# RMSNorm with Silu on one core: Square, sum and gamma in operations of four rows, with rstd as the scale of one-row Silu

## The chip, the cores and the metric

The kernel runs on one core of a Trainium2 chip. The rounds of the experiments ran on three different chips, each beside the kernel before, so kernels of different rounds are best compared by their ratios. The metric is the time of one execution on the device in microseconds (us), as the median of the runs. Engines: ACT is ScalarE, DVE is VectorE, POOL is GpSimd, SP is SyncE, which issues the loads. The stores are issued from ACT.

## The reference

```python
# x: [16, 1024, 512] float32, gamma: ones(512), eps = 1e-5
rms = np.sqrt(np.mean(x ** 2, axis=-1, keepdims=True) + eps)
x_norm = x / rms * gamma
out = x_norm * (1.0 / (1.0 + np.exp(-x_norm)))        # Silu
```

That is 33.5 MB in and 33.5 MB out, and little arithmetic on each element.

## The kernel before

The 16,384 rows lie as 128 partitions x 128 rows. They come in tiles of 4, 4, 8, six times 16, 8 and 8 rows (per partition) into a ring of 96 rows, and are worked on in place, in 32 chunks of four rows. The schedule is written by hand: what stands in the loop is the order of each engine's instructions.

```python
def sums(k):                       # mean square: three rows on ACT, one on DVE
    for j in range(cn):            # cn = 4
        row = xb[:, chunks[k] + j, :]
        if j < n_act:              # n_act = 3
            nc.scalar.activation(out=junk, in_=row, func=AF.Square,
                                 accum_out=ms[:, k, j : j + 1])
        else:
            nc.vector.tensor_tensor_reduce(... accum_out=ms[:, k, j : j + 1])

def root(k):                       # DVE: mean + eps; POOL: to the power -0.5
    nc.vector.tensor_scalar(out=aeps[:, k, :], in0=ms[:, k, :], ...)
    nc.gpsimd.tensor_tensor(out=rstd[:, k, :], in0=aeps[:, k, :],
                            in1=neg_half[:], op=ALU.pow)

def norm(k):                       # DVE: x * rstd * gamma, row by row, in place
    for j in range(cn):
        nc.vector.scalar_tensor_tensor(out=row, in0=row,
            scalar=rstd[:, k, j : j + 1], in1=gamma_sb[:], ...)

def swish(k):                      # ACT: Silu of four rows in one operation
    nc.scalar.activation(out=rows, in_=rows, func=AF.Silu)

for k in range(K + 3):             # K = 32; [cut: guards]
    sums(k); root(k)
    # stores of finished tiles
    norm(k - 1)
    swish(k - 2)                   # and loads of further tiles
```

Of the kernel before, what the change touches and what calls it, by code (L numbers as in the profile page):

```python
# [1 line left out]

# [4 lines left out]


@with_exitstack
def kernel(  # L10
    ctx: ExitStack,
    tc: tile.TileContext,
    x: bass.AP,
    gamma: bass.AP,
    eps: bass.AP,
    out: bass.AP,
):
    nc = tc.nc
    P = nc.NUM_PARTITIONS
    AF = mybir.ActivationFunctionType  # L20
    ALU = mybir.AluOpType
    fp32 = mybir.dt.float32
    bf16 = mybir.dt.bfloat16

    xf = x.flatten_outer_dims()
    of = out.flatten_outer_dims()
    R, D = xf.shape


    sizes = [4, 4, 8] + [16] * 6 + [8, 8]  # L30
    ring = 96
    ahead = 32
    cn = 4
    n_act = 3
    N = sum(sizes)
    assert N * P == R, (N, R)


    tiles = []
    done = 0  # L40
    for sz in sizes:
        assert done % ring + sz <= ring
        tiles.append((done * P, sz, done % ring))
        done += sz
    chunks = [r for _, sz, at in tiles for r in range(at, at + sz, cn)]
    K = len(chunks)

    pool = ctx.enter_context(tc.tile_pool(name="all", bufs=1))
    junk_pool = ctx.enter_context(tc.tile_pool(name="junk", bufs=1))
    xb = pool.tile([P, ring, D], fp32, name="xb")  # L50
    gamma4 = pool.tile([P, D], fp32, name="gamma4")
    gamma_sb = pool.tile([P, D], fp32, name="gamma_sb")
    neg_half = pool.tile([P, cn], fp32, name="neg_half")
    ms = pool.tile([P, K, cn], fp32, name="ms")
    aeps = pool.tile([P, K, cn], fp32, name="aeps")
    rstd = pool.tile([P, K, cn], fp32, name="rstd")

    inv_d = 1.0 / float(D)
    eps_f = float(eps)

    def dram(ap, t):
        first, sz, _ = tiles[t]
        return ap[first : first + P * sz].rearrange("(p n) d -> p n d", n=sz)

    def buf(t):
        _, sz, at = tiles[t]
        return xb[:, at : at + sz, :]

    def load(t):
        nc.sync.dma_start(out=buf(t), in_=dram(xf, t))  # L70

    def store(t):
        nc.scalar.dma_start(out=dram(of, t), in_=buf(t))

    def sums(k):
        for j in range(cn):
            row = xb[:, chunks[k] + j, :]
            if j < n_act:
                junk = junk_pool.tile([P, D], bf16, name=f"junk_a{j}")
                nc.scalar.activation(  # L80
                    out=junk[:], in_=row, func=AF.Square,
                    accum_out=ms[:, k, j : j + 1],
                )
            else:
                junk = junk_pool.tile([P, D], bf16, name=f"junk_v{j}")
                nc.vector.tensor_tensor_reduce(  # L86
                    out=junk[:], in0=row, in1=row,
                    scale=1.0, scalar=0.0, op0=ALU.mult, op1=ALU.add,
                    accum_out=ms[:, k, j : j + 1],
                )  # L90

    def root(k):
        nc.vector.tensor_scalar(  # L93
            out=aeps[:, k, :], in0=ms[:, k, :], scalar1=inv_d, scalar2=eps_f,
            op0=ALU.mult, op1=ALU.add,
        )
        nc.gpsimd.tensor_tensor(  # L97
            out=rstd[:, k, :], in0=aeps[:, k, :], in1=neg_half[:], op=ALU.pow
        )

    def norm(k):
        for j in range(cn):
            row = xb[:, chunks[k] + j, :]
            nc.vector.scalar_tensor_tensor(  # L104
                out=row, in0=row, scalar=rstd[:, k, j : j + 1],
                in1=gamma_sb[:], op0=ALU.mult, op1=ALU.mult,
            )

    def swish(k):
        rows = xb[:, chunks[k] : chunks[k] + cn, :]  # L110
        nc.scalar.activation(out=rows, in_=rows, func=AF.Silu)  # L111

    with tc.manual_schedule():
        nc.gpsimd.memset(gamma4[:], 0.0)  # L114
        nc.gpsimd.memset(neg_half[:], -0.5)  # L115
        nc.scalar.dma_start(out=gamma4[0:P:32, :], in_=gamma.partition_broadcast(4))
        nc.scalar.preload_act_table_set("silu_and_others")  # L117

        loaded = 0
        rows_loaded = 0  # L120
        while rows_loaded < ahead:
            load(loaded)
            rows_loaded += tiles[loaded][1]
            loaded += 1

        ends = []
        e = 0
        for _, sz, _ in tiles:
            e += sz // cn
            ends.append(e)  # L130
        stored = 0
        for k in range(K + 3):
            if k < K:
                sums(k)
                root(k)
            while stored < len(tiles) and ends[stored] <= k - 2:
                store(stored)
                stored += 1
            if k == 0:
                nc.vector.stream_shuffle(gamma_sb[:], gamma4[:], [0] * 32)  # L140
            if 1 <= k <= K:
                norm(k - 1)
            if 2 <= k < K + 2:
                swish(k - 2)
                while loaded < len(tiles) and ends[loaded] <= k - 1 + ahead // cn + 2:
                    load(loaded)
                    loaded += 1


# [1 line left out]
_INS = ['x', 'gamma', 'eps']  # L151
_OUTS = [((16, 1024, 512), 'float32')]

_NUMBERS = {'eps': 9.999999747378752e-06}


# [26 lines left out]
```

## Time and profile before

| | before |
|---|---|
| median time | 163.06 us (three runs, 162.83 to 163.09) |
| span in the profile | 161.1 us |
| bytes moved, mean rate | 67.15 MB, 417 GB/s |
| DMA per chunk of four rows | 2.1 MB, about 5.0 us at that rate |
| compute per chunk while data is there | 3.64 us |

These are lines of the page of the kernel before: the busy time of each engine, then two rows of the 40 equal slices of the span (tenths busy of the DMA engines, and GB/s), then the line of the chain of waits that gives its parts by line (a q behind an engine's name means its queue of instructions).

```profile
DVE 110.7 (69%) x226; ACT 118.7 (74%) x225; POOL 46.4 (29%) x38
DMA  5999989999899999999999999999999999999993
GB/s 171 437 435 521 390 352 488 413 403 480 366 407 431 484 411 447 399 456 447 399 447 456 399 439 464 417 415 421 431 435 464 419 403 472 415 415 423 439 415 146
...
DMA xb<-in_x_dram 41%; DMA out_dram<-xb 19%; ACT junk_a L80 12%; ACT xb L111 8%; DVE xb L104 3%; SPq L70 1%; DVEq L178 0%; DVE aeps L93 0%; ACTq L80 0%
```

The DMA engines are at 8 tenths or more from the second slice to the last but one; the two compute engines are busy for about 70% only. The chain that ended last is mostly transfers. So DMA is the limit. The longest waits of ACT and DVE (engine, line and tile, what it waited for, us in total, times, longest) agree:

```profile
ACT junk_a L80 <- DMA xb<-in_x_dram: 23.9, 7, 6.9
DVE junk_v L86 <- DMA xb<-in_x_dram: 19.6, 5, 5.8
```

ACT and DVE stand still for loads for some 20 us each. The timeline shows what a chunk costs where data is there (start us, duration us, engine, line, operation, out<-in, shape, count; in brackets the idle time before it and what ended it). Here and below, lines that the reading does not need are left out between those shown. The first two lines are from the start of the kernel:

```profile
7.63 0.72 DVE L140 STREAM_SHUFFLE gamma_sb<-gamma 128x512 f32<-128x512 f32 x1
7.84 1.01 POOL L97 TENSOR_TENSOR rstd<-aeps,neg_half 128x4 f32<-128x4 f32 x1 [6.55 <-DVE aeps L93]
...
110.51 0.17 DVE L93 TENSOR_SCALAR aeps<-ms 128x4 f32<-128x4 f32 x1 [0.22 <-ACT junk_a L80]
110.59 2.73 DVE L104 SCALAR_TENSOR_TENSOR xb<-xb,rstd,gamma_sb 128x512 f32<-128x512 f32 x4
110.76 1.44 POOL L97 TENSOR_TENSOR rstd<-aeps,neg_half 128x4 f32<-128x4 f32 x1 [2.20 <-DVE aeps L93]
114.15 0.17 DVE L93 TENSOR_SCALAR aeps<-ms 128x4 f32<-128x4 f32 x1 [0.22 <-ACT junk_a L80]
```

The eps operation comes again after 114.15 - 110.51 = 3.64 us. Look also at the pow on POOL. Beside the shuffle, which has one input, it takes 1.01 us; beside the multiply by rstd and gamma, which has two inputs in SBUF (the on-chip memory of the operands), it takes 1.44 us. In this kernel nothing waits long for it.

### The profile page before, as it was taken

The page shows a single profiled execution, that of the slowest core. Times are in us where ns is not written, and L with a number is a line of the kernel's source. Part 1 is how long each engine was busy: PE and PEld are TensorE (multiplying, and loading weights), DVE is VectorE, ACT ScalarE, POOL GpSimd, SP SyncE. Part 2 cuts the span into 40 slices and gives each one's busy share as a digit, 9 for nine tenths or more (in the row PEclk, how much of TensorE's full clock was granted, in tenths as well). Part 3 has the DMA queues.
Part 4 walks back from the last instruction along what each step waited for, and adds up shares of the span by engine and source line. Part 5 has one row for each costly group of instructions (what it writes and reads, how often), then busy time and mean ns, then how long its engine had stood idle before and what let it go on. Part 6 is the DMA issues. An engine that isn't in the chain of part 4 may idle for free.

```text
span 161.1 us, 612 instructions
## 1 busy us (share of the span) xinstructions
DVE 110.7 (69%) x226; ACT 118.7 (74%) x225; POOL 46.4 (29%) x38
## 2 busy tenths in 40 slices
DVE  0376946998999999999966998069999604990000
ACT  3447919999999999999939996099999408954000
POOL 1052403333444433333333333033333302400000
DMA  5999989999899999999999999999999999999993
GB/s 171 437 435 521 390 352 488 413 403 480 366 407 431 484 411 447 399 456 447 399 447 456 399 439 464 417 415 421 431 435 464 419 403 472 415 415 423 439 415 146
DMA packets 3180, 67.15 MB, mean 417 GB/s; under 512 B 356, under 2 KB 356, under 8 KB 360
## 3 DMA queue, kind: packets, MB, share of 16 engines
q1 hardware_dynamic: 1584, 33.56, 49.1%
q10 hardware_dynamic: 1592, 33.56, 48.4%
q14 instruction: 4, 0.03, 0.0%
HBM read 33.56 MB, written 33.55 MB: 417 GB/s over the span
## 4 chain that ended last, share of the span: by engine, by line
DMA 59%; ACT 20%; another core or an unknown queue 4%; issue 4%; DVE 3%; SPq 1%; DVEq 0%; ACTq 0%
DMA xb<-in_x_dram 41%; DMA out_dram<-xb 19%; ACT junk_a L80 12%; ACT xb L111 8%; DVE xb L104 3%; SPq L70 1%; DVEq L178 0%; DVE aeps L93 0%; ACTq L80 0%
## 5 line engine op out<-in xcount | busy, mean ns | idle before, releaser
L104 DVE SCALAR_TENSOR_TENSOR xb<-xb,rstd,gamma_sb 128x512 f32<-128x512 f32 x128 | 87.4, 745 | 0.0
L80 ACT ACTIVATE junk_a<-xb 128x512 bf16<-128x512 f32 x96 | 59.0, 615 | 23.9 <-DMA xb<-in_x_dram 23.9
L97 POOL TENSOR_TENSOR rstd<-aeps,neg_half 128x4 f32<-128x4 f32 x32 | 45.6, 1426 | 94.1 <-DVE aeps L93 94.1
L111 ACT ACTIVATE xb<-xb 128x2048 f32<-128x2048 f32 x32 | 60.7, 1896 | 1.8 <-DVE xb L104 1.8
L86 DVE CUSTOM_DVE_ANT_0 junk_v<-xb 128x512 bf16<-128x512 f32 x32 | 21.9, 685 | 19.6 <-DMA xb<-in_x_dram 19.6
L80 ACT ACTIVATION_READ_ACCUMULATOR junk_a<-xb 128x1 f32 x96 | 18.0, 187 | 0.0
L93 DVE TENSOR_SCALAR aeps<-ms 128x4 f32<-128x4 f32 x32 | 5.4, 170 | 14.5 <-ACT junk_a L80 14.5
L117 ACT ACT_TABLE_LOAD x1 | 1.3, 1283 | 2.4 <-issue 2.4
L86 DVE DVE_READ_ACCUMULATOR2_ANT ms<- 128x1 f32 x32 | 2.6, 82 | 0.0
L140 DVE STREAM_SHUFFLE gamma_sb<-gamma 128x512 f32<-128x512 f32 x1 | 0.7, 725 | 0.0
L114 POOL MEMSET gamma<- 128x512 f32 x1 | 0.5, 524 | 0.3 <-POOLq L164 0.3
L164 POOL MEMSET const-float32-0.0<- 128x1 f32 x1 | 0.1, 98 | 0.2 <-issue 0.2
L164 POOL MEMSET const-bfloat16-1.0<- 128x1 bf16 x1 | 0.1, 101 | 0.0
L164 POOL MEMSET const-uint8-127<- 128x1 uint8 x1 | 0.1, 101 | 0.0
L115 POOL MEMSET neg_half<- 128x4 f32 x1 | 0.1, 101 | 0.0
L164 POOL MEMSET const-float32-1.0<- 128x1 f32 x1 | 0.1, 98 | 0.0
L140 DVE LOAD_MASK_SELECT gamma_sb<-gamma x1 | 0.0, 14 | 0.0
## 6 DMA issues: line engine op xcount, KB each, us to landing
xb<-in_x_dram SPq DMA_DIRECT2D x6, 4096.0 KB, 43.8
out_dram<-xb ACTq DMA_DIRECT2D x6, 4096.0 KB, 34.6
xb<-in_x_dram SPq DMA_DIRECT2D x3, 2048.0 KB, 38.8
out_dram<-xb ACTq DMA_DIRECT2D x3, 2048.0 KB, 13.9
xb<-in_x_dram SPq DMA_DIRECT2D x2, 1024.0 KB, 5.8
out_dram<-xb ACTq DMA_DIRECT2D x2, 1024.0 KB, 19.7
gamma<-in_gamma_dram ACTq DMA_DIRECT2D x1, 8.0 KB
```

Source lines behind the costliest of these rows:

```text
L70: nc.sync.dma_start(out=buf(t), in_=dram(xf, t))
L80: nc.scalar.activation(out=junk[:], in_=row, func=AF.Square, accum_out=ms[:, k, j : j + 1],)
L86: nc.vector.tensor_tensor_reduce(out=junk[:], in0=row, in1=row, scale=1.0, scalar=0.0, op0=ALU.mult, op1=ALU.add, accum_out=ms[:, k, j : j ...
L93: nc.vector.tensor_scalar(out=aeps[:, k, :], in0=ms[:, k, :], scalar1=inv_d, scalar2=eps_f, op0=ALU.mult, op1=ALU.add,)
L97: nc.gpsimd.tensor_tensor(out=rstd[:, k, :], in0=aeps[:, k, :], in1=neg_half[:], op=ALU.pow)
L104: nc.vector.scalar_tensor_tensor(out=row, in0=row, scalar=rstd[:, k, j : j + 1], in1=gamma_sb[:], op0=ALU.mult, op1=ALU.mult,)
L111: nc.scalar.activation(out=rows, in_=rows, func=AF.Silu)
L114: nc.gpsimd.memset(gamma4[:], 0.0)
L115: nc.gpsimd.memset(neg_half[:], -0.5)
L117: nc.scalar.preload_act_table_set("silu_and_others")
L140: nc.vector.stream_shuffle(gamma_sb[:], gamma4[:], [0] * 32)
L164: nc = _bacc.Bacc("TRN2", target_bir_lowering=False, num_devices=1)
```

## The change

The intent is to have fewer, larger operations: one Square of four rows on ACT into PSUM (a second on-chip memory), one sum of them on DVE, one multiply by gamma on DVE that no longer needs rstd, and rstd as the scale of Silu, which then runs row by row on ACT. It is meant to save the fixed cost of many small operations (before, a Square of 512 columns takes 615 ns on ACT, a Silu of 2048 columns 1896 ns, less than four times that) and of the accumulator reads (187 ns each on ACT, 96 of them). The loop's order is changed too: Square(k) now stands behind Silu(k-2) on ACT, where it stood behind Silu(k-3) before.

```diff
+    def square(k):
+        squares[k] = squares_pool.tile([P, cn, D], fp32, name="sq")   # PSUM, 2 buffers
+        nc.scalar.activation(
+            out=squares[k][:], in_=rows(k), func=AF.Square, scale=inv_d**0.5
+        )
     def sums(k):
-        for j in range(cn): ...            # three Squares on ACT, one on DVE  [cut]
+        nc.vector.tensor_reduce(
+            out=ms[:, k, :], in_=squares.pop(k)[:], op=ALU.add,
+            axis=mybir.AxisListType.X,
+        )
-    def norm(k):
-        for j in range(cn): ...            # row * rstd * gamma  [cut]
+    def scaled(k):
+        nc.vector.tensor_tensor(
+            out=rows(k), in0=rows(k),
+            in1=gamma_sb[:].unsqueeze(1).to_broadcast([P, cn, D]), op=ALU.mult,
+        )
     def swish(k):
-        nc.scalar.activation(out=rows, in_=rows, func=AF.Silu)
+        for j in range(cn):
+            row = xb[:, chunks[k] + j, :]
+            nc.scalar.activation(
+                out=row, in_=row, func=AF.Silu, scale=rstd[:, k, j : j + 1]
+            )
         for k in range(K + 3):
-            sums(k); root(k)
             # stores
-            norm(k - 1)
             swish(k - 2)                   # and loads
+            square(k)
+            scaled(k)
+            sums(k)
+            root(k)
```

## The prediction

> **What bounds the kernel now.** DMA. The slices show it 9 tenths busy or more nearly throughout; 67.15 MB at a mean 417 GB/s, so about 5.0 us per chunk of four rows. Compute is faster: with data there, the timeline repeats every 3.64 us per chunk, and the waits show ACT 23.9 us and DVE 19.6 us waiting for loads. Compute ends at 146.8 us, DMA 12 us later. So the question is only whether the new schedule still fits under 5.0 us per chunk.
>
> **Engine work per chunk, after (estimates).**
> ACT: Square of 2048 about 1.85 us (Silu of 2048 is 1.895 us now)[...].[...] Sum 4.3 us (3.64 before).
> DVE: multiply about 2.25 us, sum from PSUM about 2.3 us (scaled from one 512-column operation at 683 ns per step[...]), eps about 0.15 us: 4.65 us (3.6 before). Each engine alone would fit.
>
> **The chain does not fit.** In the new order Square(k) stands behind Silu(k-2) on ACT, and the in-place multiply waits for Square(k). So there is a loop over two chunks: Square 1.85, multiply 2.25, sum 2.3, eps 0.2, pow 1.0 to 1.44,[...] and some 0.3 us of handovers: 10.3 to 10.7 us, 5.15 to 5.35 us per chunk. That alone makes compute slower than DMA.
>
> **The pow may make it worse.** Now pow takes 1.012 us once, beside a one-input shuffle, and 1.439 us otherwise, when it starts 0.17 us into a 512-column multiply with two SBUF inputs: 0.43 us more[...].[...] the trace agrees with a block to the end of one instruction. The new multiply is four times as long: if every second pow begins just behind it, it waits about 2.0 us, takes about 3.0 us, and the loop grows to about 12.3 us, 6.1 per chunk. The other pow (DVE idle then) stays near 1.0.
>
> **Time.** First chunk at 5.5 us, 32 chunks of 6.1 us, the last chain, the last 2 MB store with nothing to hide it (estimate 7 us), 2 us between span and time: about 211 us with the block, 183 to 190 us without. I give the block two chances in three. Predicted 209 us, range 182 to 218. Chances: faster 0.01, same 0.03, slower 0.96.
>
> **What would show it right.** DMA no longer full in the slices, 320 to 370 GB/s; ACT's waits for loads nearly gone, in their place Silu waiting for pow and the multiply for Square; the chain of waits through ACT, DVE and POOL, not DMA; pow in two groups, about 1.0 and 3.0 us, if the block is real, or all 1.0 to 1.45 us if not; starts of the multiply alternating between 4.7 us and 7.6 us (block) or 5.6 us (no block).
>
> **What would make it wrong.**[...] Square and multiply overlapping;[...] a phase in which no pow meets a multiply. If DVE alone set the pace, 4.65 us per chunk, it would still be about 169 us.

Some sums hold a term that is no longer listed: ACT's 4.3 us per chunk is Square's 1.85 and an estimate for four Silu, and the loop's 10.3 to 10.7 us holds the same estimate; the terms left there come to 7.9 us with a pow of 1.0 and to 8.3 with 1.44. The changed kernel then showed 2.47 us from four Silu to the next Square. The scaling of DVE's 2.25 and 2.3 us took off a fixed part; a line through 170 ns for the 4 columns of eps and 683 ns for 512, both in the trace before, gives 2.23 us for 2048. The 0.3 us of handovers and the 7 us of the last store are estimates: before, a pow starts 0.08 us after the end of its eps (110.76 in the timeline above), and in the changed kernel the span ends 7.2 us after the issue of the last store (202.64 to 209.8). For the block there is what the one trace shows: the pow's 0.43 us more, counted from its start 0.17 us into the multiply, reach to 0.60 us, near the end of that multiply's step of 0.68 us. That the wait would grow with the multiply was the estimate.

## The result, and the profile after

The changed kernel takes 211.6 us (median of 4 runs, 211.57 to 211.61) against 163.07 us before (four runs: the three above and one more). The ratio is 1.298, 95% interval 1.296 to 1.300. Ratios here and below are the mean time of one kernel's runs over the mean of the other's of the same rounds, so they are not quite the ratio of the medians quoted. The result is correct.

The same lines of the page after:

```profile
DVE 148.4 (71%) x98; ACT 138.7 (66%) x161; POOL 64.5 (31%) x38
DMA  6999999999999999999999700990029600794727
GB/s 231 439 431 431 406 437 405 470 390 459 450 425 420 406 469 425 406 469 428 400 464 428 312 0 0 400 400 0 0 100 400 300 0 0 300 400 200 300 100 300
...
POOL rstd L97 23%; DVE xb L102 17%; ACT xb L110 17%; DVE ms L87 17%; ACT sq L82 13%; DMA gamma<-in_gamma_dram 2%; DVE aeps L93 1%; POOLq L179 1%; DVE gamma_sb L145 0%; POOL gamma L115 0%; DVEq L102 0%; POOL neg_half L116 0%; DVEq L145 0%; P
```

The change did not save work on the engines: instructions fell from 612 to 395, but DVE is busy for 148.4 us (110.7 before) and ACT for 138.7 (118.7 before). DVE now sums all four rows of a chunk instead of one, and ACT runs Silu row by row.

The DMA is full up to the 22nd slice; after that it has gaps, and the waits below show that compute sets them, not the loads. Over the whole span it moves 320 GB/s, where the prediction had said 320 to 370. The chain that ended last is now pow, multiply, Silu, sum and Square, with 13% to 23% each, and the transfers of x and out have left it (the page cuts this line at its end). The waits of ACT and DVE for this circle of work, and ACT's for loads:

```profile
ACT xb L110 <- POOL rstd L97: 58.9, 16, 5.3
DVE xb L102 <- ACT sq L82: 42.7, 15, 2.9
ACT sq L82 <- DMA xb<-in_x_dram: 2.5, 2, 1.8
```

Loads are hardly waited for. ACT's Silu waits for pow, and DVE's multiply waits for Square: 16 and 15 times, so in every second chunk. One turn of the timeline shows why:

```profile
114.89 1.86 ACT L82 ACTIVATE sq<-xb 128x2048 f32<-128x2048 f32 x1
116.68 2.54 ACT L110 ACTIVATE xb<-xb,rstd 128x512 f32<-128x512 f32 x4
116.78 2.29 DVE L102 TENSOR_TENSOR xb<-xb,gamma_sb 128x2048 f32<-128x2048 f32 x1 [2.85 <-ACT sq L82]
118.98 2.28 DVE L87 TENSOR_REDUCE ms<-sq 128x4 f32<-128x2048 f32 x1
121.30 0.17 DVE L93 TENSOR_SCALAR aeps<-ms 128x4 f32<-128x4 f32 x1
121.38 2.28 DVE L102 TENSOR_TENSOR xb<-xb,gamma_sb 128x2048 f32<-128x2048 f32 x1
121.55 2.98 POOL L97 TENSOR_TENSOR rstd<-aeps,neg_half 128x4 f32<-128x4 f32 x1 [6.54 <-DVE aeps L93]
124.56 2.56 ACT L110 ACTIVATE xb<-xb,rstd 128x512 f32<-128x512 f32 x4 [3.57 <-POOL rstd L97]
126.15 1.01 POOL L97 TENSOR_TENSOR rstd<-aeps,neg_half 128x4 f32<-128x4 f32 x1 [1.62 <-DVE aeps L93]
127.03 1.86 ACT L82 ACTIVATE sq<-xb 128x2048 f32<-128x2048 f32 x1
```

Follow the circle from one Square to the Square two chunks later, by differences of the starts: Square to multiply 1.89, to sum 2.20, to eps 2.32, to pow 0.25, pow until Silu 3.01, four Silu until the next Square 2.47. The sum is 12.14 us for two chunks, 6.07 per chunk, more than the 5.0 that DMA needs. No engine is full in it: DVE is busy for 71% of the span, ACT for 66%.

The pow in the circle takes 2.98 us, the other one, at 126.15, takes 1.01 us. The long one starts 0.17 us behind the start of the next chunk's multiply.

### The profile page after: what moved, and what is told of

The parts are those of the page before. It is cut to its first block, busy times and chain, and to the rows that moved or that the text cites. A ratio compares the mean times of both kernels' runs of the same rounds, so it can differ in the third digit from the quotient of the medians. Undisturbed runs are those within 1.5% of the kernel's fastest.

```text
span 209.8 us, 395 instructions
## 1 busy us (share of the span) xinstructions
DVE 148.4 (71%) x98; ACT 138.7 (66%) x161; POOL 64.5 (31%) x38
## 4 chain that ended last, share of the span: by engine, by line
DVE 36%; ACT 30%; POOL 23%; issue 5%; DMA 2%; POOLq 1%; DVEq 0%
POOL rstd L97 23%; DVE xb L102 17%; ACT xb L110 17%; DVE ms L87 17%; ACT sq L82 13%; DMA gamma<-in_gamma_dram 2%; DVE aeps L93 1%; POOLq L179 1%; DVE gamma_sb L145 0%; POOL gamma L115 0%; DVEq L102 0%; POOL neg_half L116 0%; DVEq L145 0%; POOLq L97 0%; POOLq L165 0%
## 5 line engine op out<-in xcount | busy, mean ns | idle before, releaser
L110 ACT ACTIVATE xb<-xb,rstd 128x512 f32<-128x512 f32 x128 | 81.6, 708 | 59.0 <-POOL rstd L97 58.9
L97 POOL TENSOR_TENSOR rstd<-aeps,neg_half 128x4 f32<-128x4 f32 x32 | 63.7, 1992 | 135.0 <-DVE aeps L93 135.0
L102 DVE TENSOR_TENSOR xb<-xb,gamma_sb 128x2048 f32<-128x2048 f32 x32 | 73.2, 2289 | 42.8 <-ACT sq L82 42.7
L87 DVE TENSOR_REDUCE ms<-sq 128x4 f32<-128x2048 f32 x32 | 73.1, 2283 | 0.0
L82 ACT ACTIVATE sq<-xb 128x2048 f32<-128x2048 f32 x32 | 59.5, 1859 | 2.5 <-DMA xb<-in_x_dram 2.5
```

The lines of the kernel that those rows point to most:

```text
L82: nc.scalar.activation(out=squares[k][:], in_=rows(k), func=AF.Square, scale=inv_d**0.5)
L87: nc.vector.tensor_reduce(out=ms[:, k, :], in_=squares.pop(k)[:], op=ALU.add, axis=mybir.AxisListType.X,)
L102: nc.vector.tensor_tensor(out=rows(k), in0=rows(k), in1=gamma_sb[:].unsqueeze(1).to_broadcast([P, cn, D]), op=ALU.mult,)
L110: nc.scalar.activation(out=row, in_=row, func=AF.Silu, scale=rstd[:, k, j : j + 1])
```

## The experiments

Two things are to be told apart. LOOP is the two-chunk circle. BLOCK is the idea that a pow which meets a multiply with two SBUF inputs must wait for this one instruction. The rivals are that pow is merely slowed while DVE works (SLOW), that only the sum of engine work counts (WORK), or that blocked pows cost time wherever they are. Twelve kernels were run, all correct, each in three timed rounds beside the kernel before.

| run | what differs from the changed kernel | median us | ratio to before |
|---|---|---|---|
| (changed) | | 211.60 | 1.298 |
| split13 | multiply in 1 + 3 rows | 188.88 | 1.158 |
| split22 | multiply in 2 + 2 rows | 196.89 | 1.207 |
| sqsbuf | squares as bf16 in SBUF | 212.09 | 1.301 |
| gammapsum | sqsbuf, and gamma in PSUM | 183.19 | 1.123 |
| lag3 | Silu one chunk later | 167.51 | 1.026 |
| sumsfirst | sum and eps ahead of the multiply | 178.46 | 1.093 |
| lag3_tail | lag3, last tile cut in two | 166.72 | 1.020 |
| lag3_gammapsum | lag3 and gammapsum together | 167.80 | 1.029 |
| filler | useless memset of 384 columns behind eps | 217.17 | 1.330 |
| filler1024 | the same with 1024 columns | 227.79 | 1.397 |
| filler2048 | the same with 2048 columns | 244.89 | 1.502 |
| fillerwait | memset of 384 columns that the multiply waits for | 185.82 | 1.139 |

### Cutting the multiply: split13 and split22

```diff
-        nc.vector.tensor_tensor(out=rows(k), ...)        # four rows
+        first = chunks[k]
+        for n in (1, 3):                                 # split22: (2, 2)
+            part = xb[:, first : first + n, :]
+            nc.vector.tensor_tensor(out=part, in0=part, ...)
+            first += n
```

> The changed kernel with its multiply of four rows cut into a multiply of one row and one of three: the same elements[...]. Theory BLOCK (a pow that comes while a multiply with two SBUF inputs reads, waits until that one instruction has read all): the wait is for one row only, so pow takes about 1.44 us instead of 2.98, the two-chunk loop falls from 12.14 to about 10.7 us, time about 189 us. Rival SLOW (pow is slowed for as long as VectorE multiplies at all): pow stays near 3.0 us, time 212 to 214 us. Rival WORK (only engine work counts): 212 to 214 us.

> As split13, but cut into two multiplies of two rows. BLOCK: the first piece reads for 1024 columns, so the blocked pow takes about 1.97 us, the loop about 11.2 us, time about 197 us: between split13 and the uncut kernel, by the length of the first piece. SLOW and WORK: pow about 3.0 us, time 212 to 214 us.

Measured: 188.88 us and 196.89 us. The timeline of split13, then that of split22, at a pow that meets a multiply (the two pieces are merged into one line, x2, under the shape of the first):

```profile
128.91 2.35 DVE L105 TENSOR_TENSOR xb<-xb,gamma_sb 128x512 f32<-128x512 f32 x2
129.08 1.38 POOL L97 TENSOR_TENSOR rstd<-aeps,neg_half 128x4 f32<-128x4 f32 x1 [4.93 <-DVE aeps L93]
```

```profile
123.68 2.36 DVE L105 TENSOR_TENSOR xb<-xb,gamma_sb 128x1024 f32<-128x1024 f32 x2
123.85 1.91 POOL L97 TENSOR_TENSOR rstd<-aeps,neg_half 128x4 f32<-128x4 f32 x1 [5.47 <-DVE aeps L93]
```

The blocked pow takes 1.38, 1.91 and 2.98 us for a first piece of 512, 1024 and 2048 columns. The steps are 0.53 us for 512 columns and 1.07 us for 1024: 1.04 ns per column, the same as the multiply's own, whose pieces of 512 and 1024 columns take 0.69 and 1.22 us. So the pow waits for the one instruction in front of it, and not for DVE's work as a whole: the second piece follows at once and does not hold it up. More DVE instructions and a little more DVE work (2.35 us for the two pieces, 2.29 for the uncut multiply) made the kernel 23 us faster. SLOW and WORK fall.

### Taking the second SBUF input away: sqsbuf and gammapsum

The squares go from PSUM to SBUF as bf16 first (sqsbuf, the control), and then gamma takes their place in PSUM.

```diff
-    squares_pool = ... tc.tile_pool(name="squares", bufs=2, space=bass.MemoryType.PSUM)
+    squares_pool = ... tc.tile_pool(name="squares", bufs=2)         # both, tiles in bf16
+    gamma_ps = gamma_pool.tile([P, D], fp32, name="gamma_ps")       # gammapsum, in PSUM
+    nc.vector.tensor_copy(out=gamma_ps[:], in_=gamma_sb[:])         # gammapsum, once
-            in1=gamma_sb[:].unsqueeze(1)...
+            in1=gamma_ps[:].unsqueeze(1)...                         # gammapsum
```

> Control for gammapsum: the changed kernel with the squares as bf16 in SBUF instead of fp32 in PSUM[...]. The sum then reads one SBUF input. All theories: about as the changed kernel, 208 to 214 us, blocked pow about 2.98 us[...].

> sqsbuf, and gamma kept in PSUM, so that the multiply has one SBUF input and one PSUM input: same element count, same order of instructions. BLOCK[...]: no pow waits, all 32 pows near 1.0 us, the two-chunk loop about 10.2 us, time 181 to 185 us. If the pow is held up by anything else about the multiply (its length, or its being busy at all): pow stays at about 3.0 us, time 208 to 214 us.

Measured: 212.09 us for the control, 183.19 us for gammapsum. The timeline of gammapsum at a pow that starts beside a multiply:

```profile
125.09 2.29 DVE L104 TENSOR_TENSOR xb<-xb,gamma_ps 128x2048 f32<-128x2048 f32 x1
125.24 1.01 POOL L99 TENSOR_TENSOR rstd<-aeps,neg_half 128x4 f32<-128x4 f32 x1 [4.58 <-DVE aeps L95]
```

The multiply is as long as before (2286 ns in the mean, 2288 in the control) and stands in the same place, but one of its inputs no longer comes from SBUF, and the pow beside it takes 1.01 us. All 32 pows do (mean 1007 ns). The control shows that moving the squares changed the time by 0.2% only (its Square took 1894 ns against 1859, its sum 2278 against 2283). So in these runs a pow is blocked by a multiply that has both inputs in SBUF (2.98 us), and not by one that has one of them in PSUM (1.01 us). The block is worth 212.09 - 183.19 = 28.9 us here. Multiplies two chunks apart start at 120.48 and 130.68 in the same trace: 10.20 us for the circle, 5.1 per chunk. So the circle without the block is still slower than DMA, by little; that the kernel takes 20 us more than the kernel before has a second part. Where compute sets the pace, what lies ahead of the first chunk and behind the last one comes on top: 32 chunks of 5.1 us are 163 us, and the span is 181.4 us (the first multiply starts at 8.25).

### Opening the circle: lag3 and lag3_gammapsum

```diff
-            while stored < len(tiles) and ends[stored] <= k - 2:
+            while stored < len(tiles) and ends[stored] <= k - 3:
...                                    [cut: loop bound and load condition, moved by one too]
-            if 2 <= k < K + 2:
-                swish(k - 2)
+            if 3 <= k < K + 3:
+                swish(k - 3)
```

> The changed kernel, with Silu and store one chunk later, so that Square(k) stands behind Silu(k-3) on ScalarE (the order of the kernel before). Nothing of the block is taken away. Theory LOOP (the two-chunk circle Square, multiply, sum, eps, pow, Silu, next Square sets the pace): the circle now spans three chunks, 12.14 / 3 = 4.05 us, under VectorE's 4.60 us per chunk; VectorE sets the pace, its multiplies start every 4.60 us while data is there, every pow is blocked (about 2.98 us) and costs nothing; time 166 to 171 us. Rival (the block itself slows the kernel wherever it occurs): with all 32 pows blocked, 212 us or more.

> lag3 and gammapsum together: neither the two-chunk circle nor the block. Alone they gave 167.5 and 183.2 us. If the block costs only by way of the circle: no better than lag3, 166.5 to 168.5 us, all pows 1.0 us, VectorE busy throughout at 4.60 us per chunk. If the block still costs something behind lag3: 163 to 166 us.

Measured: 167.51 us and 167.80 us. The timeline of lag3, and the DVE row of its 40 slices:

```profile
99.50 2.29 DVE L102 TENSOR_TENSOR xb<-xb,gamma_sb 128x2048 f32<-128x2048 f32 x1
99.67 2.99 POOL L97 TENSOR_TENSOR rstd<-aeps,neg_half 128x4 f32<-128x4 f32 x1 [1.62 <-DVE aeps L93]
101.71 2.28 DVE L87 TENSOR_REDUCE ms<-sq 128x4 f32<-128x2048 f32 x1
102.69 2.56 ACT L110 ACTIVATE xb<-xb,rstd 128x512 f32<-128x512 f32 x4 [0.28 <-POOL rstd L97]
104.10 2.29 DVE L102 TENSOR_TENSOR xb<-xb,gamma_sb 128x2048 f32<-128x2048 f32 x1
```

```profile
DVE  0399999999999999999999999999999999999300
```

Now every pow but the last starts just behind a multiply and is blocked (mean of all 32: 2920 ns, against 1992 ns in the changed kernel), and the kernel is 44 us faster. Multiplies start every 104.10 - 99.50 = 4.60 us, which is the sum of its steps (multiply 2.20, sum 2.32, eps 0.08); DVE is 9 tenths busy or more from the third slice to the thirty-seventh. With the pow unblocked as well the time is the same. So a blocked pow costs nothing by itself: it costs by lying on the circle. The two causes do not add, because opening the circle removes both (in the right column the squares lie in SBUF too):

| | pow blocked | pow not blocked |
|---|---|---|
| circle over two chunks | 211.60 | 183.19 |
| circle over three chunks | 167.51 | 167.80 |

The 4.4 us that lag3 still takes over the kernel before are DVE's: 32 chunks of 4.60 us are 147 us of work in a row, with 7.5 us ahead of the first multiply and 11 us behind the last sum (pow, Silu, the last store) that nothing hides. Before, DVE was busy for 110.7 / 32 = 3.5 us per chunk, and DMA set the time.

lag3 also sorts the parts of the change. It keeps all the larger operations and only gives Silu and Square back the order that they had before. So of the 48.5 us that the change cost, 44 go back with the order alone, and the larger operations in the old order cost only 4.4. Whether the old, smaller operations would have stood the new order was not tried.

### Letting the pow run beside its own multiply: sumsfirst

```diff
-                scaled(k)
                 sums(k)
                 root(k)
+                scaled(k)
```

> The changed kernel, with VectorE's sum and eps ahead of the multiply of the same chunk. pow(k) now always starts just behind multiply(k) and is blocked each time (all 32 about 2.98 us), but it runs beside the multiply that Silu(k) must wait for anyway: circle Square 1.80 + sum 2.35 + eps to pow 0.25 + pow 2.98 + Silu 2.46 + handovers 0.1 = 9.9 us for two chunks, 4.97 per chunk; time 175 to 180 us. If blocked pows cost by their number, it would be slower than 212 us.

Measured: 178.46 us, with all 32 pows blocked (2912 to 2989 ns).

```profile
99.49 2.28 DVE L102 TENSOR_TENSOR xb<-xb,gamma_sb 128x2048 f32<-128x2048 f32 x1
99.67 2.98 POOL L97 TENSOR_TENSOR rstd<-aeps,neg_half 128x4 f32<-128x4 f32 x1 [2.36 <-DVE aeps L93]
102.68 2.56 ACT L110 ACTIVATE xb<-xb,rstd 128x512 f32<-128x512 f32 x4 [1.02 <-POOL rstd L97]
109.44 2.28 DVE L102 TENSOR_TENSOR xb<-xb,gamma_sb 128x2048 f32<-128x2048 f32 x1
```

The second multiply shown is the one two chunks later. Two chunks take 109.44 - 99.49 = 9.95 us, as the sum of the parts said (9.9). Twice as many blocked pows, and 33 us less than the changed kernel: the wait is now spent while the multiply does what Silu needs anyway. It counts what lies on the circle, not how much waiting there is.

### Making the multiply late: three misses, and what they showed

The thought was that a pow that starts ahead of the multiply is not blocked by it. That was the author's estimate; no trace had shown it. A memset without any input, put between eps and the next multiply, was to give the pow that lead.

```diff
                 root(k)
+                nc.vector.memset(spare[:], 0.0)     # [P, 384], then 1024, then 2048
```

> The changed kernel, with a useless VectorE memset of 384 columns (no SBUF input[...]) behind the eps operation, so that the next multiply starts about 0.5 us later[...]. BLOCK, first come first served: pow about 1.0 us throughout, two-chunk loop about 10.2 us, time 181 to 186 us[...]. If pow reads its operands only late in its 1.0 us: it is still blocked, 212 us or more.[...]

> filler with 1024 columns in place of 384. With 384 the pow was still blocked (3.32 us), although the multiply is recorded as starting 0.24 us after it[...].[...] If pow reads within 0.5 us of its start[...]: pow 1.0 us, circle set by VectorE, 2 x 5.2 = 10.4 us, time 185 to 190 us. If pow reads only at its end[...]: pow still blocked, about 3.6 us, circle 12.7 us, about 220 us.

> filler with 2048 columns: the multiply starts about 1.2 us after the pow, when an undisturbed pow (1.01 us) has ended.[...] pow 1.0 us, circle 2 x 5.8 = 11.6 us, time 201 to 206 us, still less than the changed kernel.[...] pow about 4.2 us, circle about 13.3 us, about 230 us.

The memset takes 378, 912 and 1765 ns. The two cases that filler1024 and filler2048 set against each other are, in terms of a trace, that a multiply blocks a pow only from about its own start (the lower time of each), or already while it is ready behind the memset (the higher one).

Measured: 217.17, 227.79 and 244.89 us. BLOCK as I had put it (first come, first served, by the starts in the trace) had the wrong sign in all three. From the timeline of filler:

```profile
99.69 3.32 POOL L98 TENSOR_TENSOR rstd<-aeps,neg_half 128x4 f32<-128x4 f32 x1 [6.54 <-DVE aeps L94]
99.93 2.23 DVE L103 TENSOR_TENSOR xb<-xb,gamma_sb 128x2048 f32<-128x2048 f32 x1
```

In the three runs the multiply starts 0.24, 0.90 and 1.97 us behind the pow (about 1.2 was expected of the last), and the pow takes 3.32, 3.99 and 5.06 us: the wait lasts until the multiply is done, however late it comes (the pow ends 0.85 to 0.86 us after the multiply's end in all three). (The expectation of filler1024 also misread the delay by the memset of 384 columns: the multiply starts 0.49 us behind eps in filler and 0.08 us in the changed kernel.) From the timeline of filler2048, two pows in a row:

```profile
90.14 1.01 POOL L98 TENSOR_TENSOR rstd<-aeps,neg_half 128x4 f32<-128x4 f32 x1 [1.62 <-DVE aeps L94]
90.43 1.76 DVE L150 MEMSET spare<- 128x2048 f32 x1 [0.37 <-issue]
92.91 2.29 DVE L103 TENSOR_TENSOR xb<-xb,gamma_sb 128x2048 f32<-128x2048 f32 x1 [0.71 <-ACT sq L83]
...
97.68 5.06 POOL L98 TENSOR_TENSOR rstd<-aeps,neg_half 128x4 f32<-128x4 f32 x1 [6.54 <-DVE aeps L94]
97.97 1.76 DVE L150 MEMSET spare<- 128x2048 f32 x1 [0.37 <-issue]
99.65 2.23 DVE L103 TENSOR_TENSOR xb<-xb,gamma_sb 128x2048 f32<-128x2048 f32 x1
```

The second pow starts at 97.68, the multiply at 99.65, two microseconds later, when an undisturbed pow would long have ended; yet the pow lasts until 102.74, about 0.9 us after the multiply's end. The memset is not what holds it: the first pow has the same memset beside it and takes 1.01 us. The difference is that in the first case the next multiply (92.91) still waits for Square, and in the second that Square has ended before the pow starts (97.12 in the same trace), so that it stands ready behind the memset. That led to a new theory, QUEUE, that a multiply which is ready behind another DVE instruction blocks the pow from before its own start, and to the last run:

```diff
                 root(k)
+                if k < K - 1:
+                    nc.vector.memset(gamma_sb[:, 0:384], 1.0)   # ones over ones
```

> filler once more, with a memset of the same 384 columns, but into the front of gamma's tile (ones over ones: right in this draw alone), so that the following multiply reads what the memset wrote and must wait for it[...]. The multiply's start moves as in filler, about 0.5 us behind eps, but it can't be queued as ready before the memset has ended. Theory QUEUE[...]: now pow comes first, 1.0 us throughout, circle about 10.3 us, time 182 to 187 us. Rival LATE (pow touches its operands later than 0.25 us after its start, whoever is queued), or a hold by the memset itself: pow blocked as in filler, about 3.3 us, time 215 to 219 us.

Measured: 185.82 us. The timeline of fillerwait:

```profile
95.41 0.38 DVE L150 MEMSET gamma_sb<- 128x384 f32 x1
95.47 1.01 POOL L97 TENSOR_TENSOR rstd<-aeps,neg_half 128x4 f32<-128x4 f32 x1 [4.18 <-DVE aeps L93]
95.89 2.29 DVE L102 TENSOR_TENSOR xb<-xb,gamma_sb 128x2048 f32<-128x2048 f32 x1
```

The memset has the same size as in filler, and the multiply starts 0.42 us behind the pow (0.24 us there). But now it reads what the memset writes: it starts 0.10 us after the memset's end, where in filler it starts 0.08 us before that end. All 32 pows take 1.01 us. The multiply, which starts while the pow runs, is not longer for it (2.29 us). The time falls by 31 us against filler. With filler1024 and filler2048, whose multiplies start much later still and yet block, the later start can't be the reason. So LATE falls, and QUEUE stands: in these runs a multiply that is ready behind another DVE instruction blocks a pow from before its own start (3.32, 3.99 and 5.06 us), and one that must still wait for that instruction's result does not (1.01 us). The memset over gamma is right only where gamma is ones, so this is a probe, not a version to use.

One thing stays open. In split13 the second piece is also ready behind the first, and still the pow (1.38 us) does not wait for it: it ends at 130.46, the second piece at 131.26. Nor does it wait for the second to fourth multiply in the kernel before (1.44 us). Why a ready multiply behind a memset blocks the pow, and one behind another multiply does not, was not tried.

### A shorter last store: lag3_tail

```diff
-    sizes = [4, 4, 8] + [16] * 6 + [8, 8]
+    sizes = [4, 4, 8] + [16] * 6 + [8, 4, 4]
```

> lag3 with the last tile of 8 rows cut into two of 4, so that the last store is 1 MB instead of 2. If VectorE sets the pace of lag3 and the last store lies bare behind it, about 2.5 us less than lag3; if the DMA queues set the time of lag3, no change beyond 0.5 us.

Measured: 166.72 us (166.09 to 166.84), 0.8 us less than lag3: between the two expectations, so inconclusive as a test of them. The profiled run was the fastest of the four, so its trace shows more than the medians do. In the traces the last store of 1 MB ends the span 5.4 us after its issue at 158.91, the one of 2 MB 7.1 us after its issue at 158.56. So half the bytes saved 1.7 us at the end and not 2.5 (1.05 MB at the 417 GB/s of the kernel before), and the added store cost some 0.35 us ahead of the last Silu. No version beat the kernel before.

## Why the prediction was right

It forecast 209 us with a range of 182 to 218; measured were 211.6.

- *DMA bounds the kernel before, with 5.0 us per chunk against 3.64 of compute.* Right; the changed kernel lost most of the time by going over 5.0 (6.07), and the rest because its start and its end are no longer hidden by DMA, as the prediction's sum had it (5.5 us ahead, the last chain and 7 us of last store behind; 7.2 us measured).
- *Engine work per chunk, ACT 4.3 and DVE 4.65 us.* Right: lag3, where DVE sets the pace, starts a multiply every 4.60 us. In the changed kernel the multiply took 2289 ns, the sum 2283 ns and eps 170 ns. Square took 1859 ns and Silu with rstd as its scale 708 ns, four of them in a row 2.56 us; ACT was busy for 138.7 us, without 1.3 us of table load 4.29 us per chunk.
- *A circle over two chunks, 10.3 to 10.7 us without the block.* Right in kind, a little high: gammapsum measures 10.20 us, 0.1 below the range, and 183.19 us, at the lower end of the 183 to 190 named for it; opening the circle alone gave 167.51 us.
- *The block, given two chances in three (the author's estimate).* Right: 12.14 us for the circle (12.3 said), blocked pows of 2.98 us (3.0 said), the others at 1.01 us, starts of the multiply alternating by 4.60 and 7.54 us (4.7 and 7.6 said).
- *The floor of 169 us if DVE alone set the pace.* Right within 1.5 us (lag3, 167.51).
- *What would make it wrong.* One case named there is a pow that is ahead of the multiply. The thought behind it was incomplete. I took a multiply to count from its start. The filler runs showed that a ready multiply blocks the pow earlier (3.32 us for a pow that starts 0.24 us ahead of it), so a small delay would not have helped.

The range of 182 to 218 us covers both cases, with the block and without, so the time alone would not have shown which of them holds. That the block is real was a bet of two in three; the lengths of the pow and split13, split22 and gammapsum decide it.

The point estimate was 2.6 us low because I had moved it down from the 211 us of the sum, towards the case without a block.

## What to carry to other kernels

Fewer and larger operations, in an order that leaves less lag, can lengthen a kernel in which no engine is full (here by 48.5 us, with DVE busy for 71% of the span): add up the circle of instructions that come back to the same engine, divide by the number of chunks it spans, and compare that with the pace you need; then add what lies ahead of the first chunk and behind the last. One more chunk of lag in one queue (44 us here) may be worth more than any saving inside an operation. Here the circle held a pow on GpSimd, and it helped to keep a long VectorE multiply with two SBUF inputs from holding it up: to cut the multiply (23 us less than the changed kernel in split13), to take one input from PSUM (28.9 us less than its control), or to order them so that the wait runs beside needed work (33 us less in sumsfirst).
